# Loading the first unit of a rotary-embedding kernel by rows in three transfers, and moving one store to another queue

## The chip, the cores and the metric

The kernel runs on one core of a Trainium2 chip. The metric is device time in microseconds, lower is better; a comparison uses the median of several executions, and a run is called fast when it is not disturbed. The kernel before took 84.64 us (84.56 to 84.78). The span in a profile is some 1.8 us shorter than the time of the same execution (83.1 against 84.86 us), so spans are compared with spans and times with times.

## The reference, cut to what matters

```python
# x: (8, 8, 1024, 64) float32, positions: 1024 integers, freqs: 32 float32, scale 0.5
angles = np.outer(positions * scale, freqs)
cos, sin = np.cos(angles), np.sin(angles)
x_first, x_second = x[..., :32], x[..., 32:]
out_first  = x_first * cos - x_second * sin
out_second = x_first * sin + x_second * cos
```

Input and output have 16.8 MB each. The arithmetic is six elementwise operations per pair of values.

## The kernel before

The tensor is cut into eight units of 2.097 MB, each seen as 128 partitions (rows) of 4096 fp32 values, 16 KB per row. Units 1 to 7 are loaded by GpSimd's queue, which casts to fp16 on the way (the page has 1024 KB written per unit). Unit 0 is loaded as fp32 by SyncE and ScalarE, half of its columns each, so that something moves before GpSimd's queue starts (SyncE's first packet starts at 1.75 us, GpSimd's at 5.06). Positions and frequencies come on ScalarE's queue.

```python
X0f = xin.tile([P, N], FP32, name="X0f")                       # P = 128, N = 4096
nc.sync.dma_start(out=X0f[:, : N // 2], in_=xv[0][:, : N // 2])
pin(nc.scalar.dma_start(out=pos_i64, in_=...))                 # 16 rows of 512 B
pin(nc.scalar.dma_start(out=freq_row, in_=freqs[None, :]))     # 128 B
pin(nc.scalar.dma_start(out=X0f[:, N // 2 :], in_=xv[0][:, N // 2 :]))
...                                                            # GpSimd loads units 1 to 7
...                                                            # VectorE and ScalarE make sinT, cosT
for i, u in enumerate((1, 2, 0, *range(3, NU))):               # NU = 8
    ...                                                        # four VectorE products and sums in fp16
    OUT = xout.tile([P, N], FP32, tag="O")                     # 4 buffers
    pin(nc.scalar.copy(out=OUT, in_=X[u]...))                  # fp16 to fp32
    (nc.gpsimd if i < NU // 2 else nc.sync).dma_start(out=ov[u], in_=OUT)
```

In the trace a row's part is one packet: each half of unit 0 is 128 packets of 8 KB, each store 128 of 16 KB. The profile counts 16 DMA engines; the trace keeps, for every packet, its queue, start, duration and size, but not its engine.

## Time and profile before

| what | value | read from |
|---|---|---|
| time, span | 84.64 us, 83.1 us | runs, profile |
| VectorE busy | 62.5 us, from 7.14 to 70.8 us, with one wait of 0.72 us in it | engine table, timeline |
| bytes read and written | 16.79 and 16.78 MB, 404 GB/s over the span | DMA rows |
| frequencies land | 5.88 us | chain of waits |
| unit 1 lands, unit 7 lands | 13.41 us, 43.24 us | landing events |
| last store issued, landed | 74.49 us, 82.19 us | timeline, landing events |

The lines of the profile that carry this stand in the prediction below. One more reading will be used again, the waits of SyncE's own DMA queue; the columns are the wait, its sum in us, how often, and the longest:

```profile
SPq L146 <- ACT OUT L145: 72.3, 4, 52.6
SPq L177 <- DMA out_dram<-OUT: 6.9, 2, 4.8
```

The second line is the end of the program, which waits for the last stores to land. The longest wait there is 4.8 us, what one unit takes at full rate. So the last two stores landed back to back, and the last one had been waiting for its predecessor, not for a computation. This is the signature of a kernel that ends when its transfers do.

### The profile page before, as it was taken

The numbers are of one execution on the slowest core, as the hardware profiler recorded it, in microseconds if no ns is written. First come the engines' busy times: TensorE is split into PE (matmuls) and PEld (weight loads), VectorE is DVE, ScalarE is ACT, GpSimd is POOL, SyncE is SP. The second block draws the span as 40 slices with busy tenths as digits, with TensorE's granted clock in tenths as the row PEclk, the third lists the DMA queues.
The fourth block names the chain that finished last, engine by engine and source line by source line (L and its number), as shares of the span: only waits on it lengthen the run. The fifth ranks groups of instructions, "written<-read, shape, count | busy, mean of one in ns | idle before, by whom it ended". The sixth has DMA issues, their size and how long they took to land.

```text
span 83.1 us, 154 instructions
## 1 busy us (share of the span) xinstructions
PE 1.1 (1%) x4; PEld 0.9 (1%) x4; DVE 62.5 (75%) x40; ACT 37.4 (45%) x12; POOL 6.7 (8%) x17
## 2 busy tenths in 40 slices
PE   0014000000000000000000000000000000000000
PEld 0013000000000000000000000000000000000000
DVE  0005999699999999999999999999999999000000
ACT  0600005999295098059129408805912950880000
POOL 4970000000002000200200200000000000000000
DMA  2799999999999999999999999999999999999990
GB/s 51 248 363 280 280 272 249 213 225 213 205 217 213 229 209 213 213 209 229 162 379 410 442 418 442 434 434 426 418 457 418 434 442 418 434 418 450 426 426 8
DMA packets 2482, 26.22 MB, mean 316 GB/s; under 512 B 290, under 2 KB 306, under 8 KB 306
## 3 DMA queue, kind: packets, MB, share of 16 engines
q0 software_dynamic: 1584, 15.73, 66.4%
q1 hardware_dynamic: 720, 9.44, 27.4%
q10 hardware_dynamic: 178, 1.06, 3.2%
HBM read 16.79 MB, written 16.78 MB: 404 GB/s over the span
## 4 chain that ended last, share of the span: by engine, by line
DVE 72%; ACT 7%; DMA 6%; DVEq 1%; PE 1%; issue 1%; ACTq 1%
DVE X L137 22%; DVE ps L136 21%; DVE X L138 12%; DVE X L141 10%; DMA freq_row<-in_freqs_dram 6%; ACT OUT L145 4%; DVE r L117 3%; DVE y L108 3%; ACT sinT L121 2%; DVE m L115 1%; DVEq L177 1%; PE cfreq L93 1%; PE pos_ps L101 1%; ACTq L66 0%; DVE posf L105 0%
## 5 line engine op out<-in xcount | busy, mean ns | idle before, releaser
L145 ACT CAST OUT<-X 128x4096 f32<-128x4096 f16 x8 | 28.8, 3605 | 25.0 <-DVE X L141 25.0
L136 DVE TENSOR_TENSOR ps<-X,sinT 128x4096 f16<-128x4096 f16 x8 | 18.3, 2284 | 0.7 <-ACT sinT L121 0.7
L137 DVE TENSOR_TENSOR X<-X,cosT 128x4096 f16<-128x4096 f16 x8 | 18.3, 2292 | 0.3
L138 DVE TENSOR_TENSOR X<-X,ps 128x2048 f16<-128x2048 f16 x8 | 9.8, 1225 | 0.3
L141 DVE TENSOR_TENSOR X<-ps,X 128x2048 f16<-128x2048 f16 x8 | 9.7, 1217 | 0.0
L121 ACT ACTIVATE sinT<-r 128x2048 f16<-128x2048 f32 x1 | 1.9, 1910 | 9.9 <-DVE r L117 9.9
L146 POOL DMA_DIRECT2D out_dram<-OUT x4 | 2.1, 534 | 39.7 <-ACT OUT L145 39.7
L74 POOL DMA_DIRECT2D X<-in_x_dram x7 | 3.9, 569 | 0.8 <-POOLq L163 0.8
L128 ACT CAST X<-X0f 128x4096 f16<-128x4096 f32 x1 | 3.6, 3589 | 0.0
L96 DVE CAST pos_row<-pos_i 16x64 f32<-16x64 int32 x1 | 0.2, 182 | 3.1 <-DMA pos_i<-in_positions_dram 3.1
L105 DVE COPY posf<-pos_ps 128x64 f32<-128x64 f32 x1 | 0.2, 224 | 2.8 <-PE pos_ps L101 2.8
L117 DVE SCALAR_TENSOR_TENSOR r<-m,y 128x2048 f32<-128x2048 f32 x1 | 2.3, 2293 | 0.0
L108 DVE TENSOR_TENSOR y<-posf,cfreq 128x2048 f32<-128x2048 f32 x1 | 2.3, 2286 | 0.0
L121 ACT ACT_TABLE_LOAD x1 | 1.3, 1283 | 2.1 <-issue 2.1
L127 ACT ACTIVATE cosT<-ra,quarter 128x2048 f16<-128x2048 f32 x1 | 2.0, 1987 | 0.0
L115 DVE TENSOR_SCALAR m<-y 128x2048 f32<-128x2048 f32 x1 | 1.2, 1226 | 0.0
L123 DVE TENSOR_SCALAR ra<-r 128x2048 int32<-128x2048 int32 x1 | 1.2, 1226 | 0.0
L89 DVE MEMSET coef<- 1x128 f32 x1 | 0.2, 165 | 0.8 <-PEq L163 0.8
L93 PE MATMUL cfreq<-freq_row,coef 1*128 1x32 f32 x2 | 0.6, 392 | 6.0 <-DMA freq_row<-in_freqs_dram 6.0
L101 PE MATMUL pos_ps<-pos_row,sel 16*128 16x64 f32 x2 | 0.7, 433 | 0.0
L93 PEld LDWEIGHTS cfreq<-freq_row,coef 1*128 1x128 f32 x2 | 0.5, 305 | 6.0 <-issue 6.0
L101 PEld LDWEIGHTS pos_ps<-pos_row,sel 16*128 16x128 f32 x2 | 0.5, 328 | 0.0
(7 smaller groups left out, 1.0 us busy)
## 6 DMA issues: line engine op xcount, KB each, us to landing
out_dram<-OUT POOLq DMA_DIRECT2D x4, 2048.0 KB, 20.5
out_dram<-OUT SPq DMA_DIRECT2D x4, 2048.0 KB, 10.8
X<-in_x_dram POOLq DMA_DIRECT2D x7, 1024.0 KB, 24.4
X0f<-in_x_dram SPq DMA_DIRECT2D x1, 1024.0 KB, 5.2
X0f<-in_x_dram ACTq DMA_DIRECT2D x1, 1024.0 KB, 11.8
pos_i<-in_positions_dram ACTq DMA_DIRECT2D x1, 8.0 KB, 3.4
freq_row<-in_freqs_dram ACTq DMA_DIRECT2D x1, 0.1 KB
```

Of the source, the lines that this page charges most:

```text
L74: nc.gpsimd.dma_start(out=X[u].rearrange("p k h j -> p (k h j)"), in_=xv[u])
L101: nc.tensor.matmul(out=pos_ps, lhsT=sel.rearrange("q a b -> q (a b)"), rhs=pos_row, start=True, stop=True)
L108: pin(nc.vector.tensor_tensor(out=y, in0=posf.unsqueeze(2).broadcast_to((P, K, half)), in1=cfreq.unsqueeze(1).broadcast_to((P, K, half)), ...
L117: pin(nc.vector.scalar_tensor_tensor(out=r, in0=m, scalar=_MAGIC, in1=y, op0=ALU.subtract, op1=ALU.subtract))
L121: pin(nc.scalar.activation(out=sinT, in_=r, func=AF.Sin, bias=0.0, scale=-_TWO_PI_DN))
L128: pin(nc.scalar.copy(out=X[0].rearrange("p k h j -> p (k h j)"), in_=X0f))
L136: pin(nc.vector.tensor_tensor(out=ps, in0=X[u], in1=sin_b, op=ALU.mult))
L137: pin(nc.vector.tensor_tensor(out=X[u], in0=X[u], in1=cos_b, op=ALU.mult))
L138: pin(nc.vector.tensor_tensor(out=X[u][:, :, 0, :], in0=X[u][:, :, 0, :], in1=ps[:, :, 1, :], op=ALU.subtract))
L141: pin(nc.vector.tensor_tensor(out=X[u][:, :, 1, :], in0=ps[:, :, 0, :], in1=X[u][:, :, 1, :], op=ALU.add))
L145: pin(nc.scalar.copy(out=OUT, in_=X[u].rearrange("p k h j -> p (k h j)")))
L146: (nc.gpsimd if i < NU // 2 else nc.sync).dma_start(out=ov[u], in_=OUT)
```

## The change

The intent, as I read it, is to get all 16 DMA engines going with a small first transfer, to use packets of 16 KB, and to give GpSimd's queue one store more.

```diff
-    nc.sync.dma_start(out=X0f[:, : N // 2], in_=xv[0][:, : N // 2])
+    pin(nc.sync.dma_start(out=X0f[0:16], in_=xv[0][0:16]))
+    pin(nc.sync.dma_start(out=X0f[16:64], in_=xv[0][16:64]))
...
-    pin(nc.scalar.dma_start(out=X0f[:, N // 2 :], in_=xv[0][:, N // 2 :]))
+    pin(nc.scalar.dma_start(out=X0f[64:P], in_=xv[0][64:P]))
...
-        (nc.gpsimd if i < NU // 2 else nc.sync).dma_start(out=ov[u], in_=OUT)
+        (nc.gpsimd if i < 5 else nc.sync).dma_start(out=ov[u], in_=OUT)
```

## The prediction

Term (c), what the row ranges cost: I put (c) at 2.2 to 4.6 us, of which 1.2 to 3.6 were for SyncE's half of unit 0, which was to end at 6.6 to 9.0 us, and about 1.0 for the third transfer. These terms were my estimates and not worked out from traces. Less (a), 0.3 to 0.7, the sum came to 1.5 to 4.3 us on top of 84.64, in the middle 3. The weights: 0.62 for (c) in full, at 86.3 to 89, and most of the rest for the first two rivals, at 83.5 to 86; weighted so, the forecast was 87.2.

> **What bounds the kernel now.** I read the page's chain of waits first, because it names a suspect, and then the DMA rows of its second part, because they contradict the chain.
>
> ```profile
> DVE 72%; ACT 7%; DMA 6%; DVEq 1%; PE 1%; issue 1%; ACTq 1%
> ```
>
> The chain follows VectorE: it starts at 7.14 us, runs without gaps, and its last product feeds ScalarE's last copy, 70.86 to 74.46. But that explains 74.5 of the 83.1 us; the rest is the last store. So I looked at what the DMA engines do over the whole span.
>
> ```profile
> DVE  0005999699999999999999999999999999000000
> ...
> DMA  2799999999999999999999999999999999999990
> GB/s 51 248 363 280 280 272 249 213 225 213 205 217 213 229 209 213 213 209 229 162 379 410 442 418 442 434 434 426 418 457 418 434 442 418 434 418 450 426 426 8
> ...
> HBM read 16.79 MB, written 16.78 MB: 404 GB/s over the span
> ```
>
> The DMA row is 9 from the third slice to the last but one: the 16 engines are never idle. The GB/s row counts bytes as they are written; units 1 to 7 are cast from fp32 to fp16 on the way in, so 213 there is 426 read. It is one rate from 6 us to 81 us. At 432 GB/s a unit of 2.097 MB takes 4.85 us, and the landings agree: units 1 to 6 land 4.85 to 4.9 us apart. Eight loads and eight stores are 16 x 4.85 = 77.6 us. The first data packet starts at 1.75 us and the last store lands at 82.2, so 80.4 us hold 77.6 us of full-rate work. Only 2.8 us are lost, and these stretches show where most of it lies:
>
> ```profile
> 1.75:4.00 2.25, 0.00 (x0) 0.00 (x0) 0.00 (x0) 1.28 (x1) 2.16 (x6) 1.00 0.91 259
> 4.00:5.00 1.00, 0.00 (x0) 0.00 (x0) 0.18 (x1) 0.00 (x0) 1.00 (x3) 1.00 0.95 401
> ...
> 40.00:42.00 2.00, 0.00 (x0) 0.00 (x0) 1.97 (x3) 0.00 (x0) 0.53 (x1) 1.00 0.87 147
> ```
>
> The last two columns are DMA share and GB/s. From 1.75 to 4.0 us the first half of unit 0 moves at about half the rate. In the packet records the 8 KB packets take 309 ns at full speed, but the first ones of the engines take 326 to 1045 ns, and several engines wait from about 2.3 to 2.9 us for their second. Sharing packets out over time, 487 KB move by 4.0 us where the full rate (422 KB per us) would move 949: 1.1 us lost. Another 0.5 us goes at 40 to 42 us, where loads turn into stores.
>
> Does the compute path also set the end? The last store is issued at 74.5 us. A first packet starts about 1.0 us after its issue (0.75 to 1.75 for unit 0), the transfer takes 4.85 and landing about 0.3, so alone it would be down at 80.6. It lands at 82.2 because the store before lands only at 77.35. The DMA engines are the bound, by 1.6 us. Time lost or won in the transfer stream goes to the end one for one; a delay of VectorE under 1.6 us goes nowhere.
>
> One more wait matters, the start of VectorE:
>
> ```profile
> 1.18 4.71 DMA freq_row<-in_freqs_dram
> ```
>
> This is 128 bytes, issued at 1.18 us and landed at 5.88. Its packet starts at 5.37, when its engine has run out of unit 0's packets of SyncE's queue. Also the first packets of GpSimd's queue (unit 1) and of unit 0's second half start at 5.06 and 5.68, each when its engine has finished SyncE's eight.[...]
>
> [...] from 57 us stores of both queues share one total of 429 GB/s.[...]
>
> [...]
>
> **The change, part by part.** Bytes do not change. (a) Unit 0's rows come as 128 packets of 16 KB instead of 256 of 8 KB. The rate of the two sizes is the same (16 KB takes 611 ns in the stores, 8 KB 309), so this saves nothing at full speed. At the start it helps: an engine's first packet is worth twice as much and bridges the wait for the second. Of the 1.1 us lost there I would credit 0.3 to 0.7.
>
> (b) SyncE issues two transfers instead of one. An issue there took 0.38 us and the second runs beside the first packet: nothing on the path.
>
> (c) [...] Sum of (c): 2.2 to 4.6 us, less (a): 1.5 to 4.3, in the middle 3.
>
> (d) Frequencies and positions wait behind SyncE's packets, so VectorE starts later by up to the first term of (c), 1.2 to 3.6 us. As the stream is as late and VectorE has 1.6 us to spare, it doesn't add.
>
> (e) Store four (counting from zero) moves to GpSimd's queue. It is the fifth; it is ready at 53.7 us. GpSimd's queue is strictly in order: its stores land at 48.2, 53.1, 58.5 and 68.2. Today store four overtakes on SyncE's queue, sharing with store three, and lands at 67.5. With the change store three lands near 63 and store four near 68 to 72, the sum of bytes unchanged. This frees store three's buffer earlier; the copy that wants it starts at 70.86 us, 2.6 us after it is free, so the wait was not there. An issue on GpSimd costs 0.53 us instead of 0.33, on an idle engine. Worth: zero, now.
>
> **The rivals.** First,[...] the start does. For: the change looks made for this,[...] the loss of 1.1 us is real; frequencies would come as early as SyncE's queue runs out.[...] It would make 84.64 - 0.6 = 84.0 us, at best 83.5; not below 82.8 even with the whole 1.1 us and some of the later losses.
>
> Second,[...] as an engine's packets are slow, those of the other two queues come in between[...]. Against: the queues alternate only once SyncE's packets have gone. It makes 84.5 to 85.5.
>
> Third, VectorE becomes the bound because the frequencies come over 1.6 us later than the stream is delayed. Its floor is 80.6 us plus their delay, at most 84.2, against 82.2 plus at least 1.5: unlikely, and inside the range anyhow.
>
> **Range and chances.**[...] Weighted, the middle lies near 87.2. Range 83.5 to 89.2. Faster by over 2% needs less than 82.95 us, that is more than the loss at the start gives back: 0.05. Within 2%: 0.34. Slower: 0.61.
>
> **What would show it.** The windows from 1.75 to 8 us decide. Right: packets of SyncE's queue of 1.2 to 2.4 us instead of 0.61,[...] the frequencies landing after 6.6, unit 1 after 15 us instead of 13.4, and every later landing late by the same amount. Wrong: 16 KB packets at 611 ns from the second on, the frequencies before 5.4 us, unit 1 at or before 13.4. The stores should land 4.85 us apart as now, the last on SyncE's queue with the one before still running at its issue. If that one has gone, VectorE has become the bound and my one-for-one reckoning fails. If the time moves while unit 1 lands when it did, the split of the stores did it, which I hold to be worth nothing.

## The result, and the profile after

The changed kernel took 89.79 us (89.34 to 90.36, 5 runs), against 84.64: slower by a factor of 1.060 (95% interval 1.055 to 1.066). All ratios here are the mean time of one kernel's fast runs over that of the other's of the same rounds, so not quite the ratio of the medians that are quoted. The prediction was 87.2, with a range up to 89.2: the direction was right, the size was not, and the measured time lies above the range.

The chain of waits of the changed kernel has a new second member:

```profile
DVE 61%; DMA 20%; ACT 4%; issue 1%; DVEq 1%; ACTq 0%; POOLq 0%
```

In the same chain, told in order of time (start, duration, what), that member is one piece:

```profile
1.26 17.72 DMA X<-in_x_dram
```

This is the load of unit 1, issued at 1.26 us as before, and landed at 18.98 instead of 13.41. VectorE's last preparation ends at 14.4 us, the sines are there at 15.1, and then it waits for it. The group of its first product shows the wait in its last column (the columns are line, engine, operation, operands and shapes, count, then busy time, mean ns, and the idle time in front with what ended it):

```profile
L137 DVE TENSOR_TENSOR ps<-X,sinT 128x4096 f16<-128x4096 f16 x8 | 18.3, 2284 | 4.7 <-DMA X<-in_x_dram 4.7
```

The rows over 40 slices of the span, VectorE's, the DMA engines' busy tenths and what they wrote:

```profile
DVE  0008995039999999999999999999999999000000
...
DMA  2989989999999999999999999999999999999992
GB/s 52 190 119 119 208 208 238 238 216 212 227 205 212 223 208 223 216 201 238 201 216 313 424 454 424 409 454 424 432 432 424 454 409 424 447 417 447 432 409 112
```

The DMA row is all but as full as before. It must be read together with the row below: in the third and fourth slice, 4.4 to 8.8 us, the engines are busy and write 119 GB/s, where the kernel before wrote 280 to 363. A busy share counts an engine that is stuck on a packet. From the ninth slice on the two kernels load alike.

The same early stretches, first of the kernel before, then of the changed one (start and end, length, busy time of five engines, TensorE's clock, DMA share, GB/s written, each packet booked at its start):

```profile
1.75:5.00 3.25, 0.00 (x0) 0.00 (x0) 0.18 (x1) 1.28 (x1) 3.16 (x8) 1.00 0.92 302
5.00:9.00 4.00, 1.08 (x4) 0.92 (x4) 1.83 (x2) 0.00 (x0) 0.68 (x2) 1.00 1.07 293
```

```profile
1.75:5.00 3.25, 0.00 (x0) 0.00 (x0) 0.00 (x0) 1.28 (x1) 3.16 (x8) 1.00 1.02 164
5.00:9.00 4.00, 1.08 (x4) 0.92 (x4) 2.18 (x3) 0.00 (x0) 0.68 (x2) 1.00 0.99 131
```

From 5 to 9 us the changed kernel writes 131 GB/s in fp32 with a DMA share of 0.99. The packet records say which packets these are:

```
transfer                 packets  start us      each takes us     all 16 engines together
rows 0-15    (SyncE)        16    1.97-2.40     0.97-1.33         
rows 16-63   (SyncE)        48    3.24, 5.25, 7.2 on (three rounds of 16)   1.91-2.05   133 GB/s
rows 64-127  (ScalarE)      64    10.8 on (four rounds, unit 1's in between) 0.74-1.23
for comparison, 16 KB packets of the stores: 0.61
```

The time to landing tells the same. Of the kernel before (out<-in, queue, count, KB, us from issue to landing):

```profile
X0f<-in_x_dram SPq DMA_DIRECT2D x1, 1024.0 KB, 5.2
X0f<-in_x_dram ACTq DMA_DIRECT2D x1, 1024.0 KB, 11.8
```

and of the changed kernel, where the 768 KB of the second transfer take 10.0 us:

```profile
X0f<-in_x_dram ACTq DMA_DIRECT2D x1, 1024.0 KB, 16.3
X0f<-in_x_dram SPq DMA_DIRECT2D x1, 768.0 KB, 10.0
X0f<-in_x_dram SPq DMA_DIRECT2D x1, 256.0 KB, 4.7
```

**Where the 5 us come from.** I add up the bytes of all packets (loads at the size read, 16 KB per row; a packet under way counts in part) and compare with a stream that starts at 1.75 us and runs at the full 422 KB per us. The difference, divided by that rate, is how far the stream lags, in us:

```
at us            5.0    10.0    18.0    39.0    44.0    75.0
before          1.09    1.18    1.25    1.30    1.83    1.88
changed         2.15    5.42    7.03    7.10    7.11    7.15
```

Up to 10 us, SyncE's rows, the changed kernel loses 5.42 - 1.18 = 4.24 us. From 10 to 18 us, ScalarE's rows beside unit 1, another 1.54. Between 39 and 44 us the kernel before loses 0.5 us that the changed one doesn't. With 0.02 elsewhere that is 5.28 (7.11 - 1.83). The last store lands at 87.12 against 82.19, 4.93 later; most of the remaining 0.35 is that before, one engine finished 0.3 us after the rest, and after the change all finish close together. The lag never falls again in either kernel: a loss in the stream is not made good.

The end is still set by the transfers: the last line of the waits of SyncE's queue in the changed kernel reads

```profile
SPq L178 <- DMA out_dram<-OUT: 8.0, 2, 4.8
```

with the same 4.8 us. VectorE ends 3.8 us later than before (74.6 against 70.8) and this doesn't set the time: the last store is issued at 78.32, and the one before it lands only at 82.27.

### The profile page after: what moved, and what is told of

It reads as the page before. It is cut to its first block, busy times and chain, and to the rows that moved or that the text cites. A ratio compares the mean times of both kernels' runs of the same rounds, so it can differ in the third digit from the quotient of the medians.

```text
span 88.0 us, 156 instructions
## 1 busy us (share of the span) xinstructions
PE 1.1 (1%) x4; PEld 0.9 (1%) x4; DVE 62.5 (71%) x40; ACT 37.5 (43%) x12; POOL 7.2 (8%) x18
## 3 DMA queue, kind: packets, MB, share of 16 engines
q10 hardware_dynamic: 114, 1.06, 4.8%
## 4 chain that ended last, share of the span: by engine, by line
DVE 61%; DMA 20%; ACT 4%; issue 1%; DVEq 1%; ACTq 0%; POOLq 0%
DVE X L138 21%; DVE ps L137 20%; DMA X<-in_x_dram 20%; DVE X L139 11%; DVE X L142 9%; ACT OUT L146 4%; DVEq L178 1%; ACTq L146 0%; DVEq L138 0%; DVEq L137 0%; POOLq L164 0%
## 5 line engine op out<-in xcount | busy, mean ns | idle before, releaser
L147 POOL DMA_DIRECT2D out_dram<-OUT x5 | 2.7, 534 | 50.0 <-ACT OUT L146 50.0
```

The source lines that it names most:

```text
L147: (nc.gpsimd if i < 5 else nc.sync).dma_start(out=ov[u], in_=OUT)
```

## The experiments

Theory: a transfer whose rows lie together in a part of the 128 has slow packets, and all of the loss comes from that. My reason why a range should be slow was shown by no run. Rivals: the store split, the number of transfers, the small first one, and the 16 KB packets. Thirteen kernels ran, all on one core; each was compared with the kernel before on the same chip, whose medians there were 84.56 to 84.65 us. All results were correct.

| run | unit 0 | stores | time us | ratio (95%) |
|---|---|---|---|---|
| e1 | rows 16, 48, 64 | 4 and 4 | 90.21 | 1.067 (1.064 to 1.070) |
| e2 | as before | 5 and 3 | 84.56 | 1.000 (0.998 to 1.001) |
| e3 | columns 1/8, 3/8, 1/2 | 4 and 4 | 85.93 | 1.014 (1.010 to 1.017) |
| e4 | rows 64, 64 | 4 and 4 | 88.02 | 1.040 (1.034 to 1.045) |
| e5 | one transfer of 128 rows | 4 and 4 | 85.49 | 1.010 (1.008 to 1.013) |
| e6 | four transfers, every fourth row | 4 and 4 | 85.25 | 1.008 (1.005 to 1.010) |
| e7 | rows 16, 16, 16, 16, 64 | 4 and 4 | 92.55 | 1.092 (1.086 to 1.098) |
| e8 | as e7, middle two exchanged | 4 and 4 | 92.26 (three fast runs) | 1.090 (1.082 to 1.097) |
| e9 | rows 32, 32, 64 | 4 and 4 | 87.19 | 1.029 (1.027 to 1.032) |
| e10 | columns 1/4, 1/4, 1/2 | 5 and 3 | 85.22 | 1.007 (1.005 to 1.009) |
| e11 | one transfer; last unit stored in halves | 5 and 3 | 84.63 | 1.001 (0.998 to 1.003) |
| e12 | both halves first on their queues; last unit in halves | 5 and 3 | 88.89 | 1.050 (1.047 to 1.052) |
| e13 | rows 32, 48, 48 | 4 and 4 | 89.47 | 1.057 (1.054 to 1.060) |

### Which part of the change (e1, e2)

e1 is the change without its last line:

```diff
-        (nc.gpsimd if i < 5 else nc.sync).dma_start(out=ov[u], in_=OUT)
+        (nc.gpsimd if i < NU // 2 else nc.sync).dma_start(out=ov[u], in_=OUT)
```

> Unit 0 by rows (16, 48, 64) as in the change, stores four and four as before. Theory ([...]the store split nothing): 89.8 us like the whole change, packets of SyncE's second transfer about 1.97 us each, unit 1 landing near 19 us. Rival (the store split costs part of it): clearly under 89.3 us.

It took 90.21 us, with packets of up to 2.03 us, and unit 1 landed at 18.85. The rows alone make the whole loss. It is 0.4 us above the changed kernel, but the two ran at different times and their intervals (1.064 to 1.070, 1.055 to 1.066) overlap, so I don't read a gain of the store split in it.

e2 is that last line alone, on the kernel before.

> Only the store split of the change (five and three), loads as before. Theory: 84.6 us, within 0.3. Rival (the fifth store behind the others in GpSimd's queue delays the end): 85 us or more; a second rival (it frees a buffer earlier): under 84.2.

It took 84.56 us, ratio 1.000. Counting from zero, store three landed at 62.58 us (68.23 before) and store four at 70.47 (67.50 before); the last landed at 82.01, as if nothing had changed. In this saturated stream the order of the stores was worth nothing.

### Row ranges or transfers (e3, e4)

```diff
# e3: on the kernel before
-    nc.sync.dma_start(out=X0f[:, : N // 2], in_=xv[0][:, : N // 2])
+    pin(nc.sync.dma_start(out=X0f[:, : N // 8], in_=xv[0][:, : N // 8]))
+    pin(nc.sync.dma_start(out=X0f[:, N // 8 : N // 2], in_=xv[0][:, N // 8 : N // 2]))
# e4: on the kernel before
+    pin(nc.sync.dma_start(out=X0f[0:64], in_=xv[0][0:64]))      # instead of the first half of columns
+    pin(nc.scalar.dma_start(out=X0f[64:P], in_=xv[0][64:P]))    # instead of the second
```

> Unit 0 in three transfers of the same bytes as in the change (1/8, 3/8, 1/2), but by columns over all 128 partitions, in packets of 2, 6 and 8 KB. Theory: [...]no slow packets, 84 to 85 us. Rival (the third transfer or the small first one costs the time, not the rows): 87 us or more.

e3 took 85.93 us: it has the change's three transfers and their bytes, and a quarter of the change's loss. No packet is slow as those of the row ranges are (packets of 6 KB take 0.23 us). I expected 85 at most, so something else cost 1.3. The landings of the last store show it: fifteen engines report between 81.29 and 81.70 us (81.27 to 81.92 in the kernel before, the last at 82.19), and one at 82.88. In the packet records, five 6 KB packets of SyncE's second transfer run late, one every 1.15 us from 5.73 to 10.35, taking turns with the other queues, when all others of that transfer are done. The records don't name engines, so that the two belong together is inferred: one engine fell 1.2 us behind in the first microseconds, and 70 us of full queues later it was still 1.2 us behind.

> Two transfers of 64 rows of 16 KB instead of 16, 48 and 64. Theory: [...]a packet costs 1.0 to 1.2 us as the third transfer's do in the change (median 1.03), SyncE's half ends near 6.5 us and the time is 86 to 87.5 us, between the two kernels. Rival (64 rows are dealt out like 48, sixteen neighbouring rows at a time[...]): packets of 2 us and 89 us or more. Rival (rows don't matter, only the small first transfer): 84.6.

e4 took 88.02 us, between the two kernels as the theory has it, if 0.5 above the 86 to 87.5 that was expected. Once under way, its packets take 1.30 us, all of them, and its windows are

```profile
1.75:5.00 3.25, 0.00 (x0) 0.00 (x0) 0.25 (x1) 1.28 (x1) 3.16 (x8) 1.00 1.04 244
5.00:9.00 4.00, 1.08 (x4) 0.93 (x4) 0.72 (x2) 0.00 (x0) 0.66 (x2) 1.00 0.95 205
```

Sixteen packets of 16 KB in 1.30 us are 202 GB/s. Both rivals fall: the rows matter without a small first transfer, and 64 rows don't behave like 48.

### Packet size, few rows, and how rows are dealt out (e5 to e8)

```diff
# e5: the only transfer of unit 0
+    pin(nc.sync.dma_start(out=X0f[:], in_=xv[0][:]))
# e6: two on SyncE, two on ScalarE
+    pin(nc.sync.dma_start(out=X0f[0:P:4], in_=xv[0][0:P:4]))
+    pin(nc.sync.dma_start(out=X0f[1:P:4], in_=xv[0][1:P:4]))
+    pin(nc.scalar.dma_start(out=X0f[2:P:4], in_=xv[0][2:P:4]))
+    pin(nc.scalar.dma_start(out=X0f[3:P:4], in_=xv[0][3:P:4]))
# e7: rows 0:16, 16:32, 32:48, 48:64 on SyncE, 64:P on ScalarE
# e8: rows 0:16, 32:48, 16:32, 48:64 on SyncE, 64:P on ScalarE
```

> Unit 0 in one transfer of 128 rows of 16 KB from SyncE. Theory[...]: packets of 0.61 us after the first, as in the stores; 84.3 to 85 us. Rival (16 KB packets are what is slow in loads): 86 us or more.

e5 took 85.49. Its packets are as expected: after the first round 0.61 to 0.64 us, but for one of 0.71. 16 KB packets are not slow. What it lost lies elsewhere, and the waits of SyncE's queue show it at once:

```profile
SPq L176 <- DMA out_dram<-OUT: 5.5, 1, 5.5
```

One wait instead of two, and longer than 4.8: the last store did not find its predecessor still running. The frequencies queued behind more of unit 0 and landed at 7.84 instead of 5.88 us, VectorE ended 2.0 us later (72.75), the last store was issued at 76.46 instead of 74.49, and the DMA engines ran dry: the lag grows from 1.66 at 75 us to 2.77 at 78. Here VectorE sets the end. This checks the prediction's figure that VectorE has 1.6 us to spare: its floor, 80.6 us plus a delay of 2.0, gives 82.6, and the last store landed at 82.71.

> Unit 0 in four transfers of 32 rows of 16 KB, each taking every fourth partition[...]; two from SyncE, two from ScalarE. Theory: few rows per transfer are harmless[...]; packets near 0.61 us[...]; 84 to 86 us. Rival (a transfer with few rows is slow by itself, or 16 KB packets are): packets of 2 us as in the change's second transfer and 88 us or more.

e6 took 85.25, with 32 rows per transfer. SyncE's packets that start before 3.7 us take 0.61 to 1.39 us, all later ones 0.61 to 0.64, most of them 0.624:

```profile
1.75:5.00 3.25, 0.72 (x4) 0.75 (x4) 0.18 (x1) 1.28 (x1) 3.16 (x8) 1.00 0.92 249
5.00:9.00 4.00, 0.36 (x2) 0.17 (x1) 3.54 (x3) 0.00 (x0) 0.68 (x2) 1.00 1.00 324
```

Few rows in a transfer are harmless when they are spread. Of all runs this speaks most directly for where the rows lie: the same 16 KB packets and fewer rows than the change's 48, at three times the speed. One caution belongs here. In every run row p of unit 0 goes from its place in DRAM to partition p, so no run tells whether a range of rows is slow where it is read or where it is written, and what it meets there was not shown.

> The change's 48 rows cut into three transfers of 16 rows, in order: 0:16, 16:32, 32:48, 48:64, then 64 rows from ScalarE. It tells how the 48 rows are dealt out. If row after row goes to the next engine, [...]packets of 1.97 us and 89.8 us. If each engine had three neighbouring rows, [...]this differs by over 0.5 us.

> The same four transfers of 16 rows with the middle two exchanged[...]. Theory: [...]the second packets take 2.3 to 2.5 us and the time is 0.3 to 1.5 us above the one in order. Rival (each step is bound by [...]16 rows being close together in memory): the same time as in order, within 0.3.

They took 92.55 and 92.26 us. They answer less than was hoped, because the packets of the later transfers of 16 rows began so late that unit 1's packets got in between. The second transfers can be compared, though. In e7, rows 16 to 31 after rows 0 to 15, a packet takes 2.19 to 2.23 us, 117 to 119 GB/s; in the change, the first round after the same rows 0 to 15 takes 1.91 to 2.02. That speaks against the change's first round of the 48 being rows 16 to 31, and so against the 48 rows going round the engines one by one. In e8, where rows 32 to 47 come second, a packet takes 2.38 to 2.42 us, about 109 GB/s for the sixteen; but e8's profile fell in a slow run (93.04 us against 91.56 at best), and the fast times of e7 and e8 overlap, so it was not shown that the order of the transfers matters.

### What sets the pace (e9, e13)

```diff
# e9
+    pin(nc.sync.dma_start(out=X0f[0:32], in_=xv[0][0:32]))
+    pin(nc.sync.dma_start(out=X0f[32:64], in_=xv[0][32:64]))
+    pin(nc.scalar.dma_start(out=X0f[64:P], in_=xv[0][64:P]))
# e13
+    pin(nc.sync.dma_start(out=X0f[0:32], in_=xv[0][0:32]))
+    pin(nc.sync.dma_start(out=X0f[32:80], in_=xv[0][32:80]))
+    pin(nc.scalar.dma_start(out=X0f[80:P], in_=xv[0][80:P]))
```

> Three transfers as in the change, but of 32, 32 and 64 rows. If each engine gets neighbouring rows (two here, three of the 48), [...]as with 64 rows: packets of about 1.3 us and the time of the two halves of 64 rows, 88.0 us within 0.7. If rows go round the engines one by one, [...]2.0 to 2.4 us a packet and 89.8 us or more. If it is the smallness of the first two transfers[...], the time is near 90 as well, but with packets of 1.3 us.

e9 took 87.19 us, 0.1 below the range that was expected, with packets of 1.26 to 1.31 us once under way. Going round the engines would have run sixteen neighbouring rows together, and those took 2.19 to 2.23 us a packet in e7. Of the two dealings, neighbouring rows for each engine (here two) is the one that fits; the records name neither engine nor row, so it is inferred. Its windows:

```profile
1.75:5.00 3.25, 0.00 (x0) 0.00 (x0) 0.00 (x0) 1.28 (x1) 3.16 (x8) 1.00 1.07 250
5.00:9.00 4.00, 1.08 (x4) 0.92 (x4) 2.17 (x3) 0.00 (x0) 0.67 (x2) 1.00 1.03 227
```

It is 0.8 us faster than e4 (lag at 3 us: 0.61 against 0.77): two smaller transfers in front did no harm.

With neighbouring rows, each engine would hold three of the change's 48, and their packets take 1.91 to 2.05 us against 1.26 to 1.31 here. e13 asked whether that comes from which rows they are or from there being 48, by moving the same shape.

> SyncE loads rows 0 to 31 and 32 to 79, ScalarE rows 80 to 127.[...] Theory[...]: packets of 1.2 to 1.35 us here instead of 1.97, SyncE's part ends near 7.4 us, and the time lies at 87 to 88.3. Rival (48 rows, three to an engine, are slow as such): 1.97 us again and 89 us or more.

The packets of rows 32 to 79 take 1.21 to 1.28 us in their first round and 1.10 to 1.18 in the next two, where those of rows 16 to 63 take 1.97. Same number of rows, same size; 48 rows are not slow as such. SyncE's part is through at 7.9 us, half a microsecond later than expected. The time, 89.47, missed my 87 to 88.3: the slow packets are now those of ScalarE's transfer, rows 80 to 127. They take 1.4 us each beside unit 1, and from 8 to 16 us the stream loses 3.2 us (lag 3.04 to 6.20), against 1.8 in e9 (2.55 to 4.33). The windows show both halves of this:

```profile
5.00:9.00 4.00, 1.08 (x4) 0.93 (x4) 2.37 (x3) 0.00 (x0) 0.67 (x2) 1.00 0.98 207
9.00:17.00 8.00, 0.00 (x0) 0.00 (x0) 5.07 (x4) 4.05 (x3) 0.00 (x0) 1.00 1.09 180
```

### Tries at a better version (e10 to e12)

```diff
# e10: columns over all partitions; stores five and three
+    pin(nc.sync.dma_start(out=X0f[:, : N // 4], in_=xv[0][:, : N // 4]))
+    pin(nc.sync.dma_start(out=X0f[:, N // 4 : N // 2], in_=xv[0][:, N // 4 : N // 2]))
# e11: e5 with stores five and three, and e11 and e12 with
+        cuts = ((0, N),) if i < NU - 1 else ((0, N // 2), (N // 2, N))
+        for a, z in cuts:
+            pin(nc.scalar.copy(out=OUT[:, a:z], in_=xf[:, a:z]))
+            (nc.gpsimd if i < 5 else nc.sync).dma_start(out=ov[u][:, a:z], in_=OUT[:, a:z])
# e12: the second half of columns is the first transfer of ScalarE's queue
+    pin(nc.scalar.dma_start(out=X0f[:, N // 2 :], in_=xv[0][:, N // 2 :]))
     pin(nc.scalar.dma_start(out=pos_i64, ...))
```

> A try at a better version that keeps the change's idea of a small first transfer: columns 1/4, 1/4, 1/2 over all partitions, stores five and three. In the column version with 1/8, 3/8, 1/2 fifteen engines finished by 81.7 us and one at 82.9[...]. If the larger first packets avoid that: 84.0 to 84.4 us. If one engine lags again: 85 to 86.

85.22 us: a miss. The engines again end apart, the last store's sixteen parts from 81.32 to 82.70 us.

> Unit 0 in one transfer from SyncE, where the frequencies came 2 us late and the DMA engines waited 1.1 us for the last unit; here the last unit is cast and stored in two halves, so that its first half is there 1.8 us earlier, and stores are five and three. If that gap at the end is what the one transfer lost: 84.2 to 84.7 us, 0.8 to 1.2 less than without halves. If the loss lies at the start: 85.3 again.

84.63 us, 0.86 less than e5 and the same as the kernel before (1.001). The gap at the end was what e5 had lost, and cutting the last unit gives it back, no more.

> Both column halves of unit 0 are the first transfers of their queues, positions and frequencies behind them on ScalarE's queue; the last unit in two halves, stores five and three. If two queues hand the engines their second packets sooner, the stream's lag behind full rate at 5 us falls from 1.1 us to 0.7 to 0.9 and the time is 84.0 to 84.5; if [...]the lag stays at 1.1 and the later frequencies (near 7.5 us) make it 84.5 to 85.5.

88.89 us, outside both expectations. The second packets came no sooner (lag at 5 us 1.10, against 1.09 before). The frequencies, now behind eight packets of their own queue that take turns with unit 1's, landed at 12.99 us instead of near 7.5, and everything on VectorE followed. It is the clearest case of a kernel bound by VectorE's start, in the waits (engine, line, what it waited for, us, times, longest):

```profile
PE cfreq L93 <- DMA freq_row<-in_freqs_dram: 13.1, 1, 13.1
```

No version beat the kernel before.

## Why the prediction was wrong in size, point by point

**The bound.** "Time lost or won in the transfer stream goes to the end one for one; a delay of VectorE under 1.6 us goes nowhere." Right. (VectorE doesn't quite run "without gaps": it waits 0.72 us for the sines at 14.5 us, which changes nothing here.) The lag grew by 5.28 us and the last landing moved by 4.93; e5 confirmed the 1.6 us.

**(a), 16 KB packets.** That the size is neutral at full speed: right, by e5. The credit of 0.3 to 0.7 us at the start: wrong. The first packets take 0.97 to 1.33 us in the change, and the lag at 3.0 us is 0.83 in both kernels. The first round is no faster, only longer.

**(b), the second issue on SyncE.** The two issues took 0.39 and 0.41 us, the second while the first packets had not begun. Right.

**(c), the row ranges.** The slow packets came as forecast, one transfer behind the other (why these rows are slow was not shown); the sum was mis-sized, and this is the step that failed. The prediction let SyncE's half end at 6.6 to 9.0 us, took the middle of the sum ("in the middle 3"), and leaned it further down with the rivals. Measured, the packets end at 9.2 to 9.6. The two transfers hardly overlap: the packets of the first end from 3.08 us on, those of the second start at 3.24, and unit 1's at 9.17, when SyncE's run out, as in the trace before (5.06). It is 1.27 + 3 x 1.97 = 7.2 us from the first start at 1.97. The upper end was the case that the order of service in the trace before pointed to, and a value in the middle had no mechanism behind it. The weighting doesn't give 87.2 either: 0.62 at the middle of 86.3 to 89 and 0.38 at the middle of 83.5 to 86 make 86.5. Against the 3.35 or so that this half took before, and with unit 1's first packets slowed to 1.06 us while the last rows drain, this term is 4.24 us instead of 1.2 to 3.6. The third DMA cost 1.54 instead of about 1.0.

So even the top of the sum was too low: 4.6 without the credit makes 89.2 us, and 5.78 (4.24 + 1.54) was lost. From the middle value to what was measured there are four shortfalls, sized roughly: no overlap instead of half of it (1.2 us), no credit (0.5), the half ending later than 9.0 with slow packets of unit 1 after it (0.6), and the third DMA (0.5). The end at 9.0 us, the case without overlap, came nearly true as a sum, but not in its parts: the working gave the first transfer more and the second less. Measured are 1.27 us from the first packet of one to that of the other, and three rounds of 1.97, 5.9 in all, at 133 GB/s.

**(d), frequencies and positions.** Wrong in its sign, without effect. The frequencies were to land after 6.6 us; their packet slipped in at 3.19, between SyncE's two transfers, and landed at 5.72, a little before the old 5.88 (2.5 us after the packet's start, where it was 0.5 before, 5.37 to 5.88). The trace before had shown the like: the 16 packets of the positions, of the same queue, ran at 2.14 to 3.04 us between SyncE's. VectorE was delayed all the same, by unit 1.

**(e), the store split.** "Worth: zero, now." Right, by e2.

**The rivals.** The first, "the start does", fell with e1 and e6. The second, that the other two queues' packets come in between, fell with the result; where other queues' packets did get in between (e7), it was slower still. "VectorE becomes the bound" didn't happen in the change, but did in e5 and e12.

**Not foreseen:** the kernel before loses 0.5 us between 39 and 42 us with load packets of up to 1.15 us, and the changed one doesn't, which took 0.5 off the loss. In e2, e3, e6, e10 and e12 it is there, in e5 and e11 smaller, in the other row versions, whose loads end later, absent. Its cause is open. Also open is why rows 16 to 63 take 1.97 us a packet and rows 32 to 79 (e13) 1.10 to 1.28, and, as said at e6, whether it happens where the rows are read or where they are written.

## What to carry to other kernels

Cut a load by columns over all 128 partitions, or by rows spread over them, not by ranges of rows: columns took 84.6 to 85.9 us (88.9 where the frequencies had to queue behind them), all or spread rows 84.6 to 85.5, ranges 87.2 to 92.6. Why a range is slow was not shown; its slow packets hold up what is queued behind them (unit 1 landed at 18.98 us instead of 13.41). When a kernel keeps the DMA engines busy from start to end, a microsecond lost at the start is paid at the end (here 4.93 of 5.28), and a DMA row full of nines says nothing about it without the GB/s beneath. When a mechanism that you trust gives a range and your own evidence on the order of service picks one end of it, predict that end; here that would have been nearer, and still low.
